# First stage of a one-core decoder trunk: filling products ahead of x, smaller first pieces, sums of squares behind the transposed x, low halves on GpSimd

## The chip, the core and the metric

The kernel runs on one core of a Trainium2 chip. TensorE (PE in the profile, its weight loads PEld), VectorE (DVE), ScalarE (ACT), GpSimd (POOL) and SyncE (SP) each work through a queue of their own in order and wait for one another by semaphores; 16 DMA engines move data. The metric is the device time of one execution in microseconds, as the median of several runs.

## The reference

The reference is a trunk of two residual layers on x of 256 tokens by 2048 features in float32, each followed by an MLP with a squared ReLU, and a norm at the end. Cut to what the change touches, the start of the first layer:

```python
D_MODEL = 2048; SEQ = 256; CONV_WIDTH = 31; EPS = 1e-6

def rms_norm(x, g):
    y = x * lax.rsqrt(jnp.mean(x * x, axis=-1, keepdims=True) + EPS)
    return y * g

def conv_module(h, w_in, b_in, dw, dw_b, ln_g, ln_b, w_out, b_out):
    u = h @ w_in + b_in                       # 2048 x 4096
    a, gate = jnp.split(u, 2, axis=-1)
    v = a * jax.nn.sigmoid(gate)
    v = depthwise causal convolution of v with dw, 31 taps, + dw_b
    v = jax.nn.silu(layer_norm(v, ln_g, ln_b))
    return v @ w_out + b_out

h = rms_norm(x, mix_norm[0])
x = x + conv_module(h, ...)
x = x + mlp(rms_norm(x, mlp_norm[0]), ...)    # then the state-space layer and its MLP
```

## The kernel before

**Precision by halves.** Products run in a one-pass float32 form that keeps fewer bits, so each operand is split: `hi` is the operand rounded to that form (an ACT copy, L117), `lo` is the operand minus `hi` (a subtraction, L119). A product is then three: hi by hi (L199), hi by the lo of the other side (L200), lo by hi (L201).

**Steps.** All weights are streamed as a list of steps, 1 MB each. `load` brings a step's chunk into one of three buffers `raw`; all chunks, and x, go through SP's queue in the order of the program (`fetch`, L91). `split` makes `hi` and `lo` of half a chunk; four buffers each for `hi` and `lo`, so splits run at most four halves ahead of the products, and a chunk can be asked for only when both halves of the chunk three before it have been split. The first two steps, halves 1 to 4 as counted in this text, are channel block 0 of `conv_w_in`, the next two, halves 5 to 8, are block 1. Each half feeds 24 products on TensorE (`mm_g`), so a block is 96. The set `pool_lo` says which steps have their `lo` made on GpSimd instead of VectorE: before the change, of `conv_in`, those from block 2 on.

**The first stage.** `setup` fetches x in four slices of 512 features, each followed by the half chunk of weights that multiplies it. TensorE transposes each slice (`to_features`, products `xt` at L242) with an identity matrix; ACT and VectorE scale it by the norm's gain `mix0` and split it into `hT` (L246, L247). The gain itself comes from a small transpose `mt` (L311) and a copy. The norm's factor per token is applied late: the sums of squares of x (`junk`, ACT at L259 and VectorE at L256) give `ssm`; GpSimd raises it to the power -1/2 (L274, `rstd`); two diagonal matrices `dg` and a product with ones (`bc`, L284) spread it over the partitions; and only the gate of block 0 (L434) uses it. In the same queue of GpSimd, behind that power, stand seven loads into one buffer `dwr`: biases and gains (L329) and the 31 convolution taps (L333). TensorE transposes them (`vt`, L335, and 16 small ones `dwt`, L341), and VectorE then starts the taps of block 0 (`cv`, L800), 30 steps per block.

**What sets the order.** The program is written once for all engines; a scheduler then sorts each engine's instructions by its own costs and by priorities (splits and gates are urgent), and inserts the waits. What an engine meets first in its queue is therefore not what stands first in the code, and any edit may move rows on all engines. `behind(ins)` tells the scheduler to place an instruction after another one.

Of the kernel before, what the change touches and what calls it, by code (L numbers as in the profile page):

```python
# [18 lines left out]
P = 128  # L19
# [17 lines left out]
class Trunk:  # L37
# [55 lines left out]
    def load(self, i, half=None):  # L93
        view, shape, _, _ = self.steps[i]
        for kind in self.before_load.pop(i, ()):
            self.table(*kind)
        if not half:
            self.raws[i] = self.w.tile(shape, F32, tag="raw", name="raw", bufs=3)
        raw = self.raws[i]
        nk = shape[1] // 2  # L100
        k = slice(0, shape[1]) if half is None else slice(half * nk, half * nk + nk)
        if len(shape) == 4:
            for j in range(shape[2]):
                self.fetch(raw[:, k, j, :], view[:, k, j, :])
        else:
            self.fetch(raw[:, k], view[:, k])
        self.loaded = i + 1

    def split(self, h, urgent=True):
# [5 lines left out]
        lo = self.w.tile([P, nk] + list(raw.shape[2:]), F32R, tag="lo", name="lo", bufs=4)  # L115
        with self.tc.high_priority(offset=URGENT if urgent else 0):
            self.nc.scalar.activation(hi, sl, AF.Copy)  # L117
            eng = self.nc.gpsimd if i in self.pool_lo else self.nc.vector
            ins = eng.tensor_tensor(out=lo, in0=sl, in1=hi.bitcast(F32), op=ALU.subtract)  # L119
            if i in self.pool_lo:  # L120
                self.pool_ins = ins
# [113 lines left out]
    def to_features(self, src, g, k0, n):  # L235

        nc = self.nc
        for k in range(k0, k0 + n, 2):
# [4 lines left out]
            for kk in range(2):  # L243
                gk = g[:, k + kk:k + kk + 1]
                h = self.hT(k + kk)
                nc.scalar.activation(h[:, 0, :], ps[:, kk, :], AF.Copy, scale=gk)  # L246
                nc.vector.scalar_tensor_tensor(out=h[:, 1, :], in0=ps[:, kk, :], scalar=gk,  # L247
                                               in1=h[:, 0, :].bitcast(F32), op0=ALU.mult, op1=ALU.subtract)
# [43 lines left out]
    def setup(self):  # L292
# [6 lines left out]
        for n in range(NS):  # L299
            s = slice(n * 512, (n + 1) * 512)  # L300
# [7 lines left out]
        nc.vector.memset(self.mhalf, -0.5)  # L308
        self.mix0 = const.tile([P, KB], F32, name="mix0")
# [5 lines left out]
        for n in range(NS):  # L315
            self.to_features(self.x, self.mix0, 4 * n, 4)
        for n in range(NS):
            self.sumsq(ssq, n, True)
# [80 lines left out]
    def conv_in(self):  # L399
# [5 lines left out]
        for c in range(KB):  # L405
            for kc in range(2):
# [9 lines left out]
                if c >= 2:  # L416
# [1095 lines left out]
```

## Time and profile before

| | |
|---|---|
| median of 3 runs | 2012.29 us (2011.23 to 2012.68) |
| the profiled execution: its time, its span | 2011.6 us, 2009.8 us |
| granted TensorE clock, mean | 0.996 |
| TensorE busy | 1977.3 us, 98% of the span |
| VectorE, ACT, GpSimd busy | 1399.2, 950.4, 280.6 us |
| DMA queue of SP | 384.85 MB, 60.9% of 16 engines over the span |
| first product of weights (L199) starts | 8.14 us |
| gate of block 0 (VectorE, L434) starts | 28.28 us |
| transposes of the taps (L341) start | 31.88 us |

The time of an execution is a little more than its span, which runs from the first to the last instruction. A row of the timeline gives start and length in us, engine, line, operation, the tile written and the tiles read, the shapes, the count, and in brackets the idle time of the engine ahead of it with what ended it. Groups give busy time and the mean of one in ns, then the idle time ahead. Matmul rows overlap in their length; the distance of their starts is what a product costs. Names are the program's: `xt` transposed x, `hT` its halves, `hi`, `lo`, `raw` as above, `dwr` the loaded constants, `acc` the accumulators.

### The profile page before, as it was taken

To read this page: it belongs to the slowest core of one execution; us is meant where nothing else is said; L and a number is where in the kernel's file an instruction comes from. 1 tells how busy PE (TensorE), PEld (TensorE's weight loads), DVE (VectorE), ACT (ScalarE), POOL (GpSimd) and SP (SyncE) were. 2 spreads that over 40 slices of the span, in tenths; PEclk is the share of its full clock that TensorE was granted. 3 is DMA by queue.
4 is the path that set the end of the run, shared out by engine and by line. 5 is a ranking of instruction groups with operands and counts; after the bars stand their busy time and mean duration, and the time that the engine had idled before them with its cause. 6 is when DMAs were issued, how large, how long until landed. Compare 5 with 4: busy or idle time off the path is not lost.

```text
span 2009.8 us, 28976 instructions
## 1 busy us (share of the span) xinstructions
PE 1977.3 (98%) x11640; PEld 1693.9 (84%) x11640; DVE 1399.2 (70%) x1905; ACT 950.4 (47%) x1172; POOL 280.6 (14%) x257
## 2 busy tenths in 40 slices
PE   8999999999999999999998999999999999999998
PEld 8999787888888888888886788888888888888887
DVE  7899899967776777776557747565556555565655
ACT  6444654444444544444443445554444444444444
POOL 3998301000000221222010000000000000000000
PEclk9999999999999999999999999999999999999999
DMA  8668458766866877877887865665656666575653
GB/s 233 190 173 217 141 199 262 229 228 191 262 189 188 220 235 245 263 249 241 321 287 269 285 210 184 194 181 186 199 187 191 188 189 195 184 223 185 198 189 126
DMA packets 317030, 428.49 MB, mean 213 GB/s; under 512 B 9761, under 2 KB 211553, under 8 KB 313537
## 3 DMA queue, kind: packets, MB, share of 16 engines
q1 hardware_dynamic: 301120, 384.85, 60.9%
q0 software_dynamic: 12352, 37.49, 6.2%
q10 hardware_dynamic: 3424, 4.30, 0.8%
q8 instruction: 91, 1.49, 0.3%
q14 instruction: 43, 0.35, 0.0%
HBM read 400.08 MB, written 34.91 MB: 216 GB/s over the span
## 4 chain that ended last, share of the span: by engine, by line
PE 92%; DVE 5%; DMA 1%; issue 1%; POOL 0%; ACT 0%; ACTq 0%; SPq 0%; POOLq 0%; DVEq 0%
PE acc L187 23%; PE acc L210 15%; PE acc L212 15%; PE acc L211 15%; PE acc L190 12%; PE acc L199 3%; PE acc L201 3%; PE acc L200 3%; DVE lo L119 1%; DVE S L791 1%; PE pk L472 1%; DMA raw<-in_conv_w_in_dram 1%; DVE ws L791 1%; PE kp L1084 0%; DMA raw<-in_mlp_w_up_dram 0%
## 5 line engine op out<-in xcount | busy, mean ns | idle before, releaser
L117 ACT ACTIVATE hi<-raw 128x1024 fp32r<-128x1024 f32 x672 | 711.8, 1060 | 968.0 <-PE acc L212 524.8
L119 DVE TENSOR_TENSOR lo<-raw,hi 128x1024 fp32r<-128x1024 f32 x612 | 747.6, 1223 | 522.2 <-ACT hi L117 513.2
L187 PE MATMUL acc<-hT,hi 128*128 128x512 f32 x2048 | 516.1, 394 | 3.0 <-DVE t L779 2.1
L187 PEld LDWEIGHTS acc<-hT,hi 128*128 128x128 f32 x2048 | 369.7, 189 | 72.2 <-DVE t L779 2.4
L210 PE MATMUL acc<-hi,rT 128*128 128x512 f32 x992 | 387.4, 391 | 0.0
L211 PE MATMUL acc<-lo,rT 128*128 128x512 f32 x992 | 386.3, 389 | 0.0
L212 PE MATMUL acc<-hi,rT 128*128 128x512 f32 x992 | 385.9, 389 | 0.0
L190 PEld LDWEIGHTS acc<-hT,lo 128*128 128x128 f32 x2048 | 279.5, 190 | 20.9 <-DVE lo L119 0.8
L190 PE MATMUL acc<-hT,lo 128*128 128x256 f32 x2048 | 286.1, 282 | 0.4 <-DVE lo L119 0.4
L210 PEld LDWEIGHTS acc<-hi,rT 128*128 128x128 f32 x992 | 186.2, 188 | 39.9 <-issue 1.8
L212 PEld LDWEIGHTS acc<-hi,rT 128*128 128x128 f32 x992 | 186.2, 188 | 39.1
L211 PEld LDWEIGHTS acc<-lo,rT 128*128 128x128 f32 x992 | 186.3, 188 | 37.8
L119 POOL TENSOR_TENSOR lo<-raw,hi 128x1024 fp32r<-128x1024 f32 x60 | 143.3, 2406 | 31.3 <-ACT hi L117 31.2
L199 PE MATMUL acc<-hT,hi 128*128 128x256 f32 x512 | 146.2, 286 | 1.1 <-ACT hi L117 1.0
L200 PE MATMUL acc<-hT,hi 128*128 128x256 f32 x512 | 145.7, 286 | 0.0
L201 PE MATMUL acc<-hT,lo 128*128 128x256 f32 x512 | 145.5, 286 | 0.0
L800 DVE SCALAR_TENSOR_TENSOR cv<-vT,dw,cv 128x256 f32<-128x256 f32 x348 | 141.2, 482 | 2.2 <-ACT cv L515 1.7
L791 DVE TENSOR_TENSOR x<-x,acc 128x1024 f32<-128x1024 f32 (+1 forms) x72 | 83.6, 1161 | 33.5 <-PE acc L212 22.8
L212 PE MATMUL acc<-hi,yT 128*128 128x512 f32 x256 | 101.7, 397 | 4.8 <-DVE yT L226 4.8
L210 PE MATMUL acc<-hi,yT 128*128 128x512 f32 x256 | 102.6, 401 | 1.3 <-ACT hi L117 1.3
L211 PE MATMUL acc<-lo,yT 128*128 128x512 f32 x256 | 101.2, 395 | 1.6 <-DVE lo L119 1.6
L199 PEld LDWEIGHTS acc<-hT,hi 128*128 128x128 f32 x512 | 98.9, 193 | 3.4 <-ACT hi L117 1.7
(274 smaller groups left out, 1732.7 us busy)
## 6 DMA issues: line engine op xcount, KB each, us to landing
raw<-in_mlp_w_up_dram SPq DMA_DIRECT2D x128, 1024.0 KB, 5.8
raw<-in_mlp_w_down_dram SPq DMA_DIRECT2D x128, 1024.0 KB, 5.2
raw<-in_ssm_w_glu_dram SPq DMA_DIRECT2D x32, 1024.0 KB, 5.5
raw<-in_conv_w_in_dram SPq DMA_DIRECT2D x60, 512.0 KB, 5.6
raw<-in_conv_w_out_dram SPq DMA_DIRECT2D x16, 1024.0 KB, 5.2
Vd<-bv POOLq DMA_DIRECT2D x16, 512.0 KB, 4.9
Md<-Kd POOLq DMA_DIRECT2D x32, 256.0 KB, 7.9
Wt<-Wd SPq DMA_DIRECT2D x8, 1024.0 KB, 8.6
```

The source lines that it names most:

```text
L117: self.nc.scalar.activation(hi, sl, AF.Copy)
L119: ins = eng.tensor_tensor(out=lo, in0=sl, in1=hi.bitcast(F32), op=ALU.subtract)
L187: mm(accs[m], lhsT=hi[:, kk, cs[m]], rhs=xT(k0 + kk), start=first and kk == 0, stop=False)
L190: mm(accs[m][:, 0:T], lhsT=lo[:, kk, cs[m]], rhs=xT(k0 + kk)[:, 0, :], start=False, stop=last and kk == 3)
L199: mm(accs[m], lhsT=hi[:, kk, c], rhs=x[:, 0, :], start=first and kk == 0, stop=False)
L200: mm(accs[m], lhsT=hi[:, kk, c], rhs=x[:, 1, :], start=False, stop=False)
L201: mm(accs[m], lhsT=lo[:, kk, c], rhs=x[:, 0, :], start=False, stop=last and kk == 3)
L210: mm(acc[:, b, :], lhsT=ak[:, 0, t], rhs=hi[:, kk, :], start=first and kk == 0, stop=False)
L211: mm(acc[:, b, :], lhsT=ak[:, 0, t], rhs=lo[:, kk, :], start=False, stop=False)
L212: self.mm_last = mm(acc[:, b, :], lhsT=ak[:, 1, t], rhs=hi[:, kk, :], start=False, stop=last and kk == 1)
L791: self.nc.vector.tensor_tensor(out=out, in0=a, in1=b, op=op)
L800: return self.nc.vector.scalar_tensor_tensor(out=out, in0=a, scalar=s, in1=b, op0=op0, op1=op1)
```

## The change

It has five parts. (1) Eight products of ones with ones, of 128 columns, are put ahead of the first transposes; their result is not used. (2) The first slice of x and its half chunk of weights come in two pieces each, and the first half is split in two pieces. (3) The sums of squares are placed behind the last instructions of the last slice's `hT`, on ACT and VectorE. (4) `pool_lo` takes in all steps of `conv_in` but the first: halves 3 to 8 have their `lo` on GpSimd. (5) `to_features` returns its last two instructions, for part 3.

```diff
-    def load(self, i, half=None):
+    def load(self, i, half=None, part=None):
...
-        if not half:
+        if not (half or part):
             self.raws[i] = self.w.tile(shape, F32, tag="raw", name="raw", bufs=3)
...
+        if part is not None:
+            k = slice(part * nk // 2, (part + 1) * nk // 2)
...
+        n = nk // 2 if h == 0 else nk
         with self.tc.high_priority(offset=URGENT if urgent else 0):
-            self.nc.scalar.activation(hi, sl, AF.Copy)
             eng = self.nc.gpsimd if i in self.pool_lo else self.nc.vector
-            ins = eng.tensor_tensor(out=lo, in0=sl, in1=hi.bitcast(F32), op=ALU.subtract)
+            for k in (slice(k, k + n) for k in range(0, nk, n)):
+                self.nc.scalar.activation(hi[:, k], sl[:, k], AF.Copy)
+                ins = eng.tensor_tensor(out=lo[:, k], in0=sl[:, k], in1=hi[:, k].bitcast(F32), op=ALU.subtract)
...
         for n in range(NS):
+            if n == 0:
+                for p in range(2):
+                    s = slice(p * 256, (p + 1) * 256)
+                    self.fetch(self.x[:, :, s], xv[:, :, s])
+                    self.load(0, 0, p)
+                continue
             s = slice(n * 512, (n + 1) * 512)
...
+        warm = self.acc2("warm")[:, 0, 0:P]
+        for _ in range(8):
+            nc.tensor.matmul(warm, lhsT=self.ones, rhs=self.ones, start=True, stop=True)
...
         for n in range(NS):
-            self.to_features(self.x, self.mix0, 4 * n, 4)
-        for n in range(NS):
-            self.sumsq(ssq, n, True)
+            ins = self.to_features(self.x, self.mix0, 4 * n, 4)
+        with self.behind(ins[0]), self.behind(ins[1]):
+            for n in range(NS):
+                self.sumsq(ssq, n, True)
...
-                if c >= 2:
+                if c or kc:
                     self.pool_lo.add(len(self.steps))
```

What the scheduler made of it, at three places. GpSimd's queue from the identity matrix on (`ssm` is the mean of squares, `dwr` the loaded constants), before:

```order
masks.py:199 AFFINE_SELECT ident<-ident 128x128
L274 TENSOR_TENSOR rstd<-ssm,mhalf 128x2
L329 DMA dwr<-in_conv_b_in_dram 32x128
L329 DMA dwr<-in_conv_dw_b_dram 16x128
L333 DMA dwr<-in_conv_dw_dram 31x2048
L119 TENSOR_TENSOR lo<-raw,hi 128x1024 x12
```

and with the change:

```order
masks.py:199 AFFINE_SELECT ident<-ident 128x128
L123 TENSOR_TENSOR lo<-raw,hi 128x1024 x4
L279 TENSOR_TENSOR rstd<-ssm,mhalf 128x2
L344 DMA dwr<-in_conv_b_in_dram 32x128
L344 DMA dwr<-in_conv_dw_b_dram 16x128
L348 DMA dwr<-in_conv_dw_dram 31x2048
L123 TENSOR_TENSOR lo<-raw,hi 128x1024 x13
```

Four low halves, 3 to 6, now stand ahead of the power and the loads (rows of the loads in between, and of memsets, are left out); the next two, 7 and 8, stand behind them.

TensorE's queue where the constants are transposed, behind products of the second block, before:

```order
L201 MATMUL acc<-hT,lo 128x256
L335 MATMUL vt<-ident,dwr 128x112
L199 MATMUL acc<-hT,hi 128x256
L200 MATMUL acc<-hT,hi 128x256
L341 MATMUL dwt<-ident,dwr 128x31 x16
```

and with the change:

```order
L204 MATMUL acc<-hT,hi 128x256
L289 MATMUL bc<-dg,ones 128x256
L350 MATMUL vt<-ident,dwr 128x112
L356 MATMUL dwt<-ident,dwr 128x31 x16
L203 MATMUL acc<-hT,hi 128x256
```

`vt` stood behind 144 products and `dwt` behind 149; both now stand behind 146, with `bc`, which stood behind 81, right ahead of them.

ACT's queue around the sums of squares (`junk`) and the diagonal `dg`, before:

```order
L259 ACTIVATE junk,ssq<-x 128x512
L246 ACTIVATE hT<-xt,mix_104 128x256
L117 ACTIVATE hi<-raw 128x1024
L246 ACTIVATE hT<-xt,mix_104 128x256 x4
L117 ACTIVATE hi<-raw 128x1024 x2
L282 ACTIVATE dg<-ident,rstd 128x128
```

and with the change:

```order
L250 ACTIVATE hT<-xt,mix_116 128x256 x4
L264 ACTIVATE junk,ssq<-x 128x512
L122 ACTIVATE hi<-raw 128x1024 x2
L264 ACTIVATE junk,ssq<-x 128x512 x3
L122 ACTIVATE hi<-raw 128x1024 x3
L287 ACTIVATE dg<-ident,rstd 128x128
```

The four sums of squares, one per slice of x before, now come after the last `hT`, three of them behind the high halves 5 and 6, and `dg` comes behind the high halves 7 to 9.

More of the change, by code (lines that the diff above doesn't have):

```diff
@@ L245, in to_features @@
                 h = self.hT(k + kk)
-                nc.scalar.activation(h[:, 0, :], ps[:, kk, :], AF.Copy, scale=gk)
-                nc.vector.scalar_tensor_tensor(out=h[:, 1, :], in0=ps[:, kk, :], scalar=gk,
-                                               in1=h[:, 0, :].bitcast(F32), op0=ALU.mult, op1=ALU.subtract)
+                hi = nc.scalar.activation(h[:, 0, :], ps[:, kk, :], AF.Copy, scale=gk)
+                lo = nc.vector.scalar_tensor_tensor(out=h[:, 1, :], in0=ps[:, kk, :], scalar=gk,
+                                                    in1=h[:, 0, :].bitcast(F32), op0=ALU.mult, op1=ALU.subtract)
+        return hi, lo
     def sumsq(self, ssq, n, both=False):
```

## The prediction

> **What bounds the kernel now.** I read the page first, then TensorE's waits, then the first 40 us by stage and by engine.
>
> ```profile
> PE 1977.3 (98%) x11640; PEld 1693.9 (84%) x11640; DVE 1399.2 (70%) x1905; ACT 950.4 (47%) x1172; POOL 280.6 (14%) x257
> PE 92%; DVE 5%; DMA 1%; issue 1%; POOL 0%; ACT 0%; ACTq 0%; SPq 0%; POOLq 0%; DVEq 0%
> ```
>
> TensorE is busy for 98% of the span and carries 92% of the chain that ended last. So only what TensorE loses counts, and a microsecond it loses early is not made up later. The change is in the start; some windows of the first 40 us (columns: length, busy time and count of PE, PEld, DVE, ACT, POOL, then clock, DMA share, GB/s):
>
> ```profile
> 5.00:10.00 5.00, 3.83 (x16) 3.43 (x17) 3.15 (x8) 3.76 (x9) 0.00 (x0) 1.00 1.06 332
> 20.00:30.00 10.00, 10.00 (x83) 9.94 (x82) 7.16 (x11) 5.43 (x8) 4.41 (x12) 1.00 1.15 258
> 30.00:40.00 10.00, 10.00 (x91) 9.83 (x90) 5.43 (x13) 8.20 (x21) 4.74 (x2) 1.00 0.99 257
> ```
>
> TensorE is full in the later two, and the DMA engines in all three (a share of about 1). What can be won is before 13.4 us:
>
> ```profile
> 8.14 0.58 PE L199 MATMUL acc<-hT,hi 128*128 128x256 f32 x1 [1.04 <-ACT hi L117]
> 8.74 1.91 PE L242 MATMUL xt<-ident,x 128*128 128x128 f32 x8
> 12.79 0.41 PE L200 MATMUL acc<-hT,hi 128*128 128x256 f32 x1
> 13.01 0.41 PE L201 MATMUL acc<-hT,lo 128*128 128x256 f32 x1
> 13.43 0.28 PE L200 MATMUL acc<-hT,hi 128*128 128x256 f32 x1
> 13.55 0.28 PE L201 MATMUL acc<-hT,lo 128*128 128x256 f32 x1
> ```
>
> Products start 0.22 us apart until 13 us and 0.12 us apart from 13.43 on: TensorE starts at half speed. The stretch from 8.74 to 13.43, 4.7 us, would take half of that at full speed. With the wait of 1.04 us before the first product, the front of the program holds at most 2.35 + 1.04 = 3.4 us.
>
> **The change, part by part.** *Filling products and smaller first pieces.* They aim at those 3.4 us. The filling runs on TensorE from about 1.2 us, when it has nothing else: no cost but a delay of the small transpose for `mix0`, which stands behind it, and of the copy that ACT's first `hT` needs. The smaller pieces put three more issues on SP's queue, each as long as this one, with the time from issue to landing of the first chunks below it:
>
> ```profile
> 0.74 0.44 SPq L91 DMA_DIRECT2D x<-in_x_dram  x1
> raw<-in_conv_w_in_dram SPq DMA_DIRECT2D x8, 256.0 KB, 6.8
> ```
>
> Three times about 0.5 us of issuing lie beside 6.8 us in which earlier bytes are still on their way, so later chunks land as before; without that cover it would be 1.5 us. Bounds for the front alone: nothing, or 3.4 us won. I take neither, because of the next part.
>
> *Low halves on GpSimd.* The chunks of the first two channel blocks, halves 3 to 8 in order, had their low halves on VectorE and now have them on GpSimd:
>
> ```profile
> L119 DVE TENSOR_TENSOR lo<-raw,hi x8: 1217/1225/1227, 8.1 to 28.9; 128x1024 fp32r<-128x1024 f32 x8
> 30.86 4.74 POOL L119 TENSOR_TENSOR lo<-raw,hi 128x1024 fp32r<-128x1024 f32 x2 [6.45 <-ACT hi L117]
> 13.37 1.06 ACT L117 ACTIVATE hi<-raw 128x1024 fp32r<-128x1024 f32 x1 [0.41 <-DMA raw<-in_conv_w_in_dram]
> 16.58 1.06 ACT L117 ACTIVATE hi<-raw 128x1024 fp32r<-128x1024 f32 x1 [0.46 <-DMA raw<-in_conv_w_in_dram]
> 20.20 2.01 ACT L117 ACTIVATE hi<-raw 128x1024 fp32r<-128x1024 f32 x2 [1.10 <-DMA raw<-in_conv_w_in_dram]
> ```
>
> One costs 1.23 us on VectorE and 2.37 us on GpSimd. Each can start only when ACT has the high half, and ACT waits for the weights to land (at 13.4, 16.6 and, for halves 5 and 6, 20.2 us). The bytes ahead of them are the same after the change and the DMA engines are full, so these landings stay. GpSimd then ends half 3 at 13.37 + 1.06 + 2.37 = 16.8, half 4 at 16.58 + 1.06 + 2.37 = 20.0, and halves 5 and 6 at 20.20 + 1.06 + 4.74 = 26.0 us. TensorE needs 24 products of 0.12 us = 2.9 us per half, so after 26.0 it is through half 6, 144 products, at about 28.9; in the profile it is there at 31.08, where the row of `vt` below starts, with the broadcast `bc` (0.4 us) already done. That is a lead of 1.8 us, however much more the front won, since half 6 sets it.
>
> *What is queued behind them on GpSimd.* The power that makes `rstd`, and behind it the seven loads of the constant vectors and convolution taps (`dwr`), now stand after these four low halves:
>
> ```profile
> 19.46 0.71 POOL L274 TENSOR_TENSOR rstd<-ssm,mhalf 128x2 f32<-128x2 f32 x1 [18.14 <-DVE ssm L272]
> 20.11 0.73 POOL L329 DMA_DIRECT2D dwr<-in_conv_b_in_dram  x1
> 23.23 0.53 POOL L333 DMA_DIRECT2D dwr<-in_conv_dw_dram  x1
> 31.08 0.26 PE L335 MATMUL vt<-ident,dwr 112*128 112x112 f32 x1
> 31.88 1.18 PE L341 MATMUL dwt<-ident,dwr 31*128 31x31 f32 x16
> 32.98 0.38 PE L201 MATMUL acc<-hT,lo 128*128 128x256 f32 x1
> ```
>
> The power started at 19.46, the last load was issued 3.77 us after that. Now the power starts at 26.0 us, 6.5 us later. The sums of squares, now behind the last transposed x, are no reason for more:
>
> ```profile
> L259 ACT ACTIVATE junk<-x 128x512 f32<-128x512 f32 x4 | 2.5, 630 | 2.6 <-DMA x<-in_x_dram 2.6
> L259 ACT ACTIVATION_READ_ACCUMULATOR junk<-x 128x1 f32 x4 | 0.8, 196 | 0.0
> ```
>
> ACT's last three come after the two high halves of 20.20, at 22.2 + 3 x 0.83 = 24.7 us, and two short VectorE steps follow. The last load is then issued at 26.0 + 3.77 = 29.8 us. TensorE's transposes of these loads (`vt`, `dwt`) stand after 146 products, where they stood after 144 and 149; TensorE reaches them at 28.9 + 0.2 + 0.4 (for `bc`, now right ahead of them) = 29.5 us and must wait, with every product queued behind. (`bc` could come later, since ACT's `dg` now stands behind the high half 9; that costs nothing of its own as long as the loads, behind `bc`, are later still.)
>
> *How long the loads take to land.* Issue to landing on GpSimd's queue, as a median or as min/median/max:
>
> ```profile
> dwr<-in_conv_dw_dram POOLq DMA_DIRECT2D x1, 248.0 KB, 7.4
> DMA to landing us min/median/max: 5.8/6.3/7.4
> DMA to landing us min/median/max: 3.3/4.0/5.0
> Kd<-zero POOLq DMA_DIRECT2D x4, 224.0 KB, 3.2
> ```
>
> The second row is all seven `dwr` loads, the third the four loads of `bo`, 256 KB each, at 101 to 123 us. The 7.4 us were taken with the DMA engines full; after the change the sixth chunk of weights can be asked for only when half 6 has been split at 26.0, and the seventh only after half 8, so about one chunk of 1 MB is in flight beside the loads. That is nearest to `bo`; since seven loads stand one behind the other I take its longest, 5.0, and keep 3.2 and 7.4 as bounds. The taps land at 29.8 + 5.0 = 34.8 us. `vt` and the 16 small transposes took 0.1 + 1.1 us: done at 36.0. Three products fewer are behind TensorE by then (3 x 0.12 = 0.36), so 36.4 against 32.98: **3.4 us lost**; by the bounds 1.6 to 5.8.
>
> *The clock after the wait.* TensorE would stand idle from 29.5 to 34.8, 5.3 us. Two waits of the profile show what follows:
>
> ```profile
> 308.52 0.50 PE L211 MATMUL acc<-lo,sT 128*128 128x512 f32 x1 [2.23 <-DVE lo L119]
> 308.85 0.39 PE L212 MATMUL acc<-hi,sT 128*128 128x512 f32 x1
> 309.08 0.40 PE L210 MATMUL acc<-hi,sT 128*128 128x512 f32 x1
> 1087.72 0.79 PE L212 MATMUL acc<-hi,yT 128*128 128x512 f32 x1 [4.83 <-DVE yT L226]
> 1088.31 0.63 PE L210 MATMUL acc<-hi,yT 128*128 128x512 f32 x1
> 1092.11 0.39 PE L210 MATMUL acc<-hi,yT 128*128 128x512 f32 x1
> ```
>
> After 2.23 us of idle time products are 0.23 us apart as before; after 4.83 us nine of them take the 3.8 us from 1088.31 to 1092.11, 0.42 each, which lost 9 x 0.2 = **1.8 us**. I take 1.8; it is nothing if the wait stays near 2 us. The Trainium skill ("TensorE: Matmul & The Clock Gate", Part 1) says that a window of about 3.4 us without work halves the clock and a busy one of that length restores it; these two waits agree, and by the rule the loss would be the same 1.7 us.
>
> *The rest.* VectorE gets 6 x 1.23 us back, in windows where it was not full (7.2 of 10 us, 5.4 of 10 us) and where nothing of TensorE's waited for it: worth nothing. Later in the program a few rows change places; the largest waits of TensorE there are these, and I leave them as they are, with 1.5 us either way in the range:
>
> ```profile
> PE acc L211 <- DVE lo L119: 3.9, 2, 2.2
> PE acc L187 <- DVE t L779: 2.1, 1, 2.1
> ```
>
> *Sum.* 3.4 + 1.8 = 5.2 us slower. The profiled execution took 2011.6 us (span 2009.8), so 2016.8; it lies 0.7 us under the median of the three runs, 2012.3, which makes **2017.5 us**. A change under 0.2%, 4.0 us, is what a measurement of this kernel cannot tell from none.
>
> **The rivals.**
>
> *The loads land soon.* At 3.2 us the taps are there at 33.0, the loss is 1.6 us, and with an idle time of 3.5 us the clock may hold: 2013.9, no measurable change. For it: one small group of transfers on this queue did land in 3.2 us. Against it: those are copies of zeros at a time of little traffic, and the same seven loads took 5.8 us or more. The Trainium skill ("DMA: Bandwidth & Descriptors", Anatomy of one DMA) gives 2.0 us plus the bytes at 436 GB/s for this path, by my estimate 2.6 us for 248 KB and a loss of 1.0 us; no load in this profile was that quick.
>
> *The lead is kept (the other side).* If the constants are there when TensorE reaches them, it keeps the lead of 1.8 us: 2010.5. It decides from a landing at 29.5, and gain and loss are equal where the taps land at 31.4 us, 1.6 us after their issue as I have it. So GpSimd would have to be done with half 6 some 2 us or more earlier than 26.0, which the landing at 20.2 and 2.37 us a piece do not allow. Even with nothing in the way, 3.4 us is below what can be told.
>
> *A second wait.* The column sums for the layer norm stand earlier in TensorE's order: the second from the start after 496 products instead of 526, 30 x 0.12 = 3.6 us. The last tap they wait for is VectorE's, and this is how far it was ahead:
>
> ```profile
> 75.11 0.48 DVE L800 SCALAR_TENSOR_TENSOR vT<-vT,dw,cv 128x256 f32<-128x256 f32 x1
> 79.13 0.62 PE L527 MATMUL stat<-vT,ones 128*32 128x256 f32 x2
> ```
>
> 3.5 us: about used up by the move. Should VectorE, which starts its taps behind the same `dwt`, come 3 us later than in the profile, 3 us more are lost: 2020.5. Against it: VectorE's order moved too, with the last tap of the first block after 46 instead of 55 of its steps.
>
> **How the numbers follow.** The stall with a fallen clock 0.64, the quick landing 0.19, the lead kept 0.06, the second wait 0.09, something else 0.02. The first reaches from 4.2 (landing in 4.0 us) to 7.8 us (in 7.4 us with 2.0 for the clock), or 2020.1; a tenth of it falls under 4.0. The range takes in the quick landing and most of the second wait, and leaves out the lead: 2012.0 to 2020.5. Faster by over 0.2%: 0.04, which is what exceeds my bound on the front. Within 0.2%: 0.19 + 0.05 + 0.07 = 0.31. Slower: 0.65.
>
> **What would show it.** Right, if in the new profile GpSimd's fourth low half ends at about 26 us, the power follows at once, TensorE has a wait of some 5 us for a `dwr` load ahead of `vt` or `dwt`, and the products behind it are 0.21 us apart for some 3.5 us. The front is right if products begin near 7 us and the halves 3 to 6 are waited for on GpSimd. I am wrong if the power starts well before 26 us, if the taps land within 3.5 us of their issue, if the clock holds through the wait, or if TensorE later has waits that the profile of before does not have.

## The result, and the profile after

The changed kernel took 2020.4 us (median of 5 executions, 2019.51 to 2025.75) against 2012.29 us: slower, by a factor of 1.0047 (95% interval 1.0033 to 1.0061). The forecast was 2017.5 us. The direction was right, and so was the kind of the loss: a wait of TensorE for the late loads, and a fallen clock behind it. Its size was not: the step that puts the power at 26.0 us failed, as worked out further down. The loss is about half as large again as forecast where a second wait stays away, and more where it comes.

The profiled execution is the longest of the five, 2025.75 us with a span of 2024.0. The busy time by engine on its page:

```profile
PE 1985.2 (98%) x11656; PEld 1700.3 (84%) x11656; DVE 1405.5 (69%) x1900; ACT 950.8 (47%) x1173; POOL 295.8 (15%) x263
```

These hardly differ from before: a page's shares cannot show 14 us in 2024. I therefore use a lag below: the start of a TensorE instruction minus the start of the same instruction in the kernel before, both from the span's start. The lag of a single row also holds any move of that row in the order. In this execution it is 1.0 us at 30 us of the time before, 9.3 us at 40, still 9.4 at 100, 14.6 at 112 and 14.3 at the end. So there are two losses, 8.3 us at 30 to 40 us and 5 us at 106 to 112, and nothing in between is made up.

The first loss, in the timeline of GpSimd, VectorE and TensorE. Low halves 5 and 6, the power and the issue of the last load on GpSimd; two of VectorE's squares; and TensorE from the broadcast on:

```profile
23.66 5.61 POOL L123 TENSOR_TENSOR lo<-raw,hi 128x1024 fp32r<-128x1024 f32 x2 [0.64 <-PE acc L205]
30.37 0.71 POOL L279 TENSOR_TENSOR rstd<-ssm,mhalf 128x2 f32<-128x2 f32 x1 [1.10 <-DVE ssm L277]
34.14 0.53 POOL L348 DMA_DIRECT2D dwr<-in_conv_dw_dram  x1
...
24.22 2.79 DVE L261 SCALAR_TENSOR_TENSOR junk<-x 128x512 f32<-128x512 f32 x1
26.94 2.88 DVE L261 SCALAR_TENSOR_TENSOR junk<-x 128x512 f32<-128x512 f32 x1
...
32.37 0.60 PE L289 MATMUL bc<-dg,ones 128*128 128x256 f32 x2
37.27 0.42 PE L350 MATMUL vt<-ident,dwr 112*128 112x112 f32 x1 [4.30 <-DMA dwr<-in_mlp_norm_dram]
37.63 1.90 PE L356 MATMUL dwt<-ident,dwr 31*128 31x31 f32 x16
39.46 0.58 PE L203 MATMUL acc<-hT,hi 128*128 128x256 f32 x1
39.84 0.41 PE L204 MATMUL acc<-hT,hi 128*128 128x256 f32 x1
44.96 0.37 PE L204 MATMUL acc<-hT,hi 128*128 128x256 f32 x1
45.16 0.28 PE L205 MATMUL acc<-hT,lo 128*128 128x256 f32 x1
```

This is the chain that the prediction describes: low halves, then the power, then the loads, then TensorE waiting at `vt`, then products 0.21 us apart until 45 us (25 of them from 39.84 to 44.96). The broadcast `bc` starts at 32.37 with no idle time of TensorE ahead of it, so neither the low halves nor the power hold TensorE there; only the load behind it does. Two things in the chain were not foreseen: half 6 ends at 29.27 instead of 26.0, and the power waits another 1.10 us for the mean of squares, since two of VectorE's squares took 2.79 and 2.88 us where one of the four took 0.68.

The second loss, by the waits of TensorE and the timeline of VectorE and GpSimd:

```profile
PE stat L542 <- DVE vT L572: 3.8, 1, 3.8
...
112.56 7.88 DVE L572 TENSOR_TENSOR vT<-vT,shift 128x1024 f32<-128x1024 f32 x1
...
112.31 2.41 POOL L403 TENSOR_TENSOR x<-x,bo 128x1024 f32<-128x1024 f32 x1
114.67 4.69 POOL L123 TENSOR_TENSOR lo<-raw,hi 128x1024 fp32r<-128x1024 f32 x2
119.31 0.56 POOL L401 DMA_DIRECT2D bo<-in_conv_b_out_dram  x1
```

The centre subtraction of the layer norm took 7.88 us; the same one took 1.67 us before. It ends at 120.44, 1.08 us after GpSimd's three operations, which end at 119.36.

### The profile page after: what moved, and what is told of

It is laid out like the page before. It is cut to its first block, busy times and chain, and to the rows that moved or that the text cites. A ratio compares the mean times of both kernels' runs of the same rounds, so it can differ in the third digit from the quotient of the medians.

```text
span 2024.0 us, 29016 instructions
## 1 busy us (share of the span) xinstructions
PE 1985.2 (98%) x11656; PEld 1700.3 (84%) x11656; DVE 1405.5 (69%) x1900; ACT 950.8 (47%) x1173; POOL 295.8 (15%) x263
## 4 chain that ended last, share of the span: by engine, by line
PE 91%; DVE 6%; issue 1%; DMA 1%; SPq 0%; POOL 0%; ACT 0%; ACTq 0%; POOLq 0%; DVEq 0%
PE acc L191 23%; PE acc L214 15%; PE acc L216 15%; PE acc L215 15%; PE acc L194 12%; PE acc L203 3%; PE acc L205 3%; PE acc L204 3%; DVE lo L123 1%; DVE S L806 1%; PE pk L487 1%; DVE ws L806 1%; PE kp L1099 0%; DMA raw<-in_mlp_w_up_dram 0%; DMA raw<-in_conv_w_in_dram 0%
## 5 line engine op out<-in xcount | busy, mean ns | idle before, releaser
L122 ACT ACTIVATE hi<-raw 128x1024 fp32r<-128x1024 f32 (+1 forms) x673 | 711.8, 1059 | 964.3 <-PE acc L216 526.9
L123 DVE TENSOR_TENSOR lo<-raw,hi 128x1024 fp32r<-128x1024 f32 (+1 forms) x607 | 740.2, 1221 | 523.4 <-ACT hi L122 522.2
L123 POOL TENSOR_TENSOR lo<-raw,hi 128x1024 fp32r<-128x1024 f32 x66 | 158.4, 2411 | 47.0 <-ACT hi L122 46.3
```

Of the source, the lines that this page charges most:

```text
L122: self.nc.scalar.activation(hi[:, k], sl[:, k], AF.Copy)
L123: ins = eng.tensor_tensor(out=lo[:, k], in0=sl[:, k], in1=hi[:, k].bitcast(F32), op=ALU.subtract)
```

## The experiments

**The changed kernel again.**

> The changed kernel once more. Two losses stand in its first profile: 8.3 us at 30 to 38 us (the wait for the constant vectors, the cold clock behind it) and 5.0 us at 107 to 122 us (a wait for a centre subtraction of 7.88 us on VectorE, which took 1.67 us before). Theory A, the first loss belongs to the change and the second to that one execution: the new profile has the wait for the vectors of 4 to 5 us again, no centre subtraction above 3 us, and a span of about 2018.5 us. Theory B, both belong to the change: the subtraction takes over 6 us again, and the span is 2022 us or more.

Measured: 2026.07 us (2019.66 to 2029.23, six executions), 1.0069 [1.0057, 1.0081].

```profile
PE vt L350 <- DMA dwr<-in_mlp_norm_dram: 4.5, 1, 4.5
...
111.18 10.76 DVE L572 TENSOR_TENSOR vT<-vT,shift 128x1024 f32<-128x1024 f32 x1
...
110.92 2.41 POOL L403 TENSOR_TENSOR x<-x,bo 128x1024 f32<-128x1024 f32 x1
113.27 4.70 POOL L123 TENSOR_TENSOR lo<-raw,hi 128x1024 fp32r<-128x1024 f32 x2
117.91 0.56 POOL L401 DMA_DIRECT2D bo<-in_conv_b_out_dram  x1
118.49 2.35 POOL L403 TENSOR_TENSOR x<-x,bo 128x1024 f32<-128x1024 f32 x1
```

Theory B holds: the first loss is there again (a wait of 4.5 us for the loads, lag 7.9 us at 40 us), and of the second 7.8 us stay (lag 16.6 at 108 us, 15.8 from 140 us to the end), against 5.0 in the first profile. This time the subtraction ended at 121.94, 1.10 us after the fourth operation on GpSimd, 120.84 (the DMA issue between them is not counted). Both belong to the change; the second varies between executions. Of its eleven times, five lie between 2019.5 and 2020.7 and six between 2023.8 and 2029.2.

**Filling and pieces alone; then one part back at a time.** Three kernels. The first has the low halves back on VectorE and the sums of squares where they were, so that only the filling and the pieces are left; the second has only the low halves back, the third only the sums. The edit for the low halves comes first, then the one for the sums:

```diff
-                if c or kc:
+                if c >= 2:
...
-            ins = self.to_features(self.x, self.mix0, 4 * n, 4)
-        with self.behind(ins[0]), self.behind(ins[1]):
-            for n in range(NS):
-                self.sumsq(ssq, n, True)
+            self.to_features(self.x, self.mix0, 4 * n, 4)
+        for n in range(NS):
+            self.sumsq(ssq, n, True)
```

> Only the filling products and the smaller pieces: low halves of the second to fourth step back on VectorE, sums of squares where they were before. Theory A (the loss is the late load of the constants, and that comes from the two other parts): no wait for a load behind 158 products; products begin near 9 us as in the changed kernel, 1 to 2 us later than before, of which the later pace of the halves hides a part: 2011.5 to 2014. Rival (the front wins, and the other parts eat the gain): products begin earlier than in the changed kernel, 2009 to 2010.5. Rival (the front itself loses what the changed kernel loses): 2016 or more.

> The changed kernel with the low halves of halves 3 to 8 back on VectorE; the sums of squares stay behind the transposed x. One low half, that of half 9, now stands ahead of the power on GpSimd, and TensorE meets the broadcast behind 190 products, the vectors behind 192. My prediction's step (low halves on GpSimd are what makes the loads late) in its plain form: nothing of the loss is left, 2011 to 2013. Theory A (the loads are late whenever the power is late, whoever makes it so): half 9 is split at about 31 us, the power comes at about 33, the last vectors land at about 41, TensorE reaches them at about 37 to 38: a wait of 3 to 4 us and a cold clock, 2016 to 2019. Theory C (GpSimd's low halves slow VectorE, and that is the loss): 2011 to 2013, with no square of VectorE above 1 us.

> The changed kernel with the sums of squares where they were; halves 3 to 8 keep their low halves on GpSimd. One low half stands ahead of the power, and TensorE meets the vectors and taps behind 76 products already. Theory A: power at about 17 us, the last load issued at about 21, landed at 27 to 28 with the DMA engines full; TensorE gets there at about 21: a wait of 5 to 7 us, then a cold clock; half 6 would have been ready at 26, so 4 to 7 us are lost against before, 2016 to 2019.5. Theory D (the two parts are only bad together, each alone is harmless): 2011 to 2013.5.

Measured, with the lag at some times of the kernel before:

| kernel | median us | ratio [95%] | lag at 30 | 40 | 100 | 140 | 356 | 400 | end |
|---|---|---|---|---|---|---|---|---|---|
| change, first profile | 2020.4 | 1.0047 [1.0033, 1.0061] | 1.0 | 9.3 | 9.4 | 14.3 | 14.0 | 14.2 | 14.3 |
| filling and pieces | 2020.28 | 1.0041 [1.0029, 1.0053] | 0.6 | 0.6 | 0.0 | 1.1 | 0.0 | 7.6 | 7.0 |
| low halves back | 2021.75 | 1.0050 [1.0038, 1.0062] | -0.4 | 3.8 | 3.7 | 4.8 | 9.9 | 10.2 | 9.8 |
| sums back | 2024.12 | 1.0061 [1.0048, 1.0074] | 8.6 | 7.2 | 7.7 | 6.9 | 9.9 | 9.0 | 13.0 |

No part undone brings the time back. In the first, the front loses nothing worth naming, as the prediction has it, and yet 7.6 us go at 356 to 400 us, where no part of the change is; no theory had that. In the second, the loads are late without any of halves 3 to 8 on GpSimd: half 9, which was on GpSimd all along, now stands ahead of the power. In the third the power is early, but the scheduler has moved `vt` up to 76 products. The rows are the power on GpSimd and TensorE's wait, for low halves back and then for sums back:

```profile
32.90 0.71 POOL L279 TENSOR_TENSOR rstd<-ssm,mhalf 128x2 f32<-128x2 f32 x1
PE vt L350 <- DMA dwr<-in_mlp_norm_dram: 1.8, 1, 1.8
...
19.55 0.71 POOL L279 TENSOR_TENSOR rstd<-ssm,mhalf 128x2 f32<-128x2 f32 x1
PE vt L349 <- DMA dwr<-in_mlp_norm_dram: 4.1, 1, 4.1
```

Theory A is right in kind in both: TensorE waits for the loads whichever part makes them late, or meets them early. Its sizes are not right: the waits are 1.8 and 4.1 us, where it had 3 to 4 and 5 to 7, and both times lie above its ranges. A part of those times is lost later: with the low halves back the lag goes from 4.8 us at 140 us to 10.7 at 280, with one wait of 2.9 us for VectorE among it; with the sums back it goes from 6.9 at 140 us to 13.0 at the end. These later losses were not traced to a cause, so neither end time is the price of a part. Low halves on GpSimd are one way to late loads, not the only one. Theories C and D fall. In these three profiles the centre subtraction took 2.17, 1.62 and 1.50 us; which part of the change brings it together with GpSimd's addition is not shown.

**Why filling and pieces alone lose 7 us.** In VectorE's order, laid beside that of the kernel before, about 150 rows at 350 us and later stand elsewhere. With one filling product fewer that part of the order is the old one again:

```diff
-        for _ in range(8):
+        for _ in range(7):
```

> Filling products and smaller pieces alone, as in the run with those two parts, but with seven filling products instead of eight: the scheduler's order on VectorE from 350 us on is then that of the kernel before, where with eight it differed by some 150 rows. Theory A (that run's loss of 7 us lies in VectorE's order at 380 to 400 us, not in the front): 2010.5 to 2013. Rival B (the front costs 6 to 8 us by itself, through late landings or ACT): 2017 to 2021, the same as with eight.

Measured: 2012.45 us, 1.0003 [0.9994, 1.0013]. The lag is about 1.0 us from 30 to 140 us and 0.1 at 400. TensorE's waits for the MLP's accumulators, and the busy times from 370 to 400 us (length, busy time and count of PE, PEld, DVE, ACT, POOL, clock, DMA share, GB/s), with eight fillings and then with seven:

```profile
PE acc L191 <- DVE t L793: 7.8, 4, 3.5
370.00:400.00 30.00, 25.29 (x137) 21.83 (x136) 30.00 (x41) 12.37 (x15) 2.53 (x3) 0.94 0.73 224
```

```profile
PE acc L191 <- DVE t L793: 3.0, 2, 2.1
370.00:400.00 30.00, 29.16 (x167) 25.46 (x166) 30.00 (x41) 15.53 (x19) 2.08 (x2) 1.00 0.88 267
```

VectorE is full in both, 30.00 of 30 us. What differs is the order of its work. The operation `t` that frees TensorE's accumulator starts at 367.7, 380.3 and 395.3 us with eight fillings, with 10, 9 and 10 operations on the next layer's tables (L805) ahead of each; with seven it starts at 365.3, 375.4 and 389.1, with 9, 4 and 9. Theory A holds: one product on an idle TensorE at 1 us decides over 7 us at 390, through the scheduler's order. The changed kernel as a whole happens not to have this loss (lag 14.0 at 356, 14.2 at 400).

**Six fillings alone.** The kernel before with six of them:

```diff
+        warm = self.acc2("warm")[:, 0, 0:P]
+        for _ in range(6):
+            nc.tensor.matmul(warm, lhsT=self.ones, rhs=self.ones, start=True, stop=True)
```

> The kernel before with six filling products and nothing else; all engines keep their order but for one place. Theory A (the landing of half 6 sets the pace of the first 30 us): the products may start at full speed, but the lag is within 0.5 us of nothing at 30 us; 2011 to 2012.5. Rival (the half-speed stretch of 8.7 to 13.4 us is really lost time): 1.5 to 2.3 us are won and stay won: 2009.5 to 2010.5.

Measured: 2011.61 us, 0.9999 [0.9990, 1.0009]. TensorE's products lead by 0.93 us until 14.0 us; from 20 to 140 us they are 0.13 to 0.15 us behind. Time and lag are as theory A has them, its reason is not: the lead is lost to a wait for VectorE's `hT`, and no wait for a half of the weights follows. With seven fillings and smaller pieces, too, the lead of 0.5 to 1.3 us ends at a wait for VectorE's `hT`. The two waits, of this run and then of that one:

```profile
14.09 0.63 PE L246 MATMUL xt<-ident,x 128*128 128x128 f32 x4 [0.63 <-DVE hT L251]
20.85 0.39 PE L204 MATMUL acc<-hT,hi 128*128 128x256 f32 x1 [0.94 <-DVE hT L251]
```

Behind these, no wait of TensorE up to the end of half 6 is above 0.15 us in either run.

**The table of ACT's functions.** The change moved ACT's first operation behind the first weights, and its table load with it. Here a small copy of a constant comes first:

```diff
         nc.vector.memset(self.mhalf, -0.5)
+        nc.scalar.activation(self.small.tile([P, NB], F32, tag="tl", name="tl", bufs=1), self.mhalf, AF.Copy)
```

> The changed kernel with one more small ACT copy of a constant at the start, which waits for no load, so that the table of ACT's functions is fetched then; all other orders are those of the changed kernel. Theory A (the table load was held up by the first weights and cost the front 1.2 us, but the front is not what decides): the first high half at about 5.7 us instead of 6.9, the first product at about 7.7 instead of 8.95; the lag against before falls by about 1.2 us at 9 to 25 us and is the same 8 to 9 us at 40 us; 2019 to 2021, or up to 2026 where the centre subtraction is held. Rival (the front carries through): the lag is lower by 1.2 us to the end.

Measured: executions of 2018.17, 2018.31, 2026.52 and 2028.34 us, 1.0064 [1.0039, 1.0089]. Table load and first product, of the changed kernel and then of this one:

```profile
5.60 1.28 ACT L122 ACT_TABLE_LOAD   x1 [5.60 <-DMA raw<-in_conv_w_in_dram]
8.95 0.58 PE L203 MATMUL acc<-hT,hi 128*128 128x256 f32 x1 [1.85 <-ACT hT L250]
```

```profile
1.23 1.28 ACT L320 ACT_TABLE_LOAD   x1 [1.23 <-PEq L1517]
7.41 0.39 PE L203 MATMUL acc<-hT,hi 128*128 128x256 f32 x1 [0.18 <-ACT hT L250]
```

The first product is 1.5 us earlier, and the lag at 40 us is 7.9 us, as in the repeated run of the change. That is as theory A has it, but it is little evidence: two profiles of the changed kernel itself differ by 1.4 us there (9.3 and 7.9), and the executions of 2018.17 and 2018.31 lie 1.2 to 2.5 us below the five of the changed kernel between 2019.5 and 2020.7. So the rival, that the 1.2 us carry through, is not excluded. In this profile the centre subtraction was not held:

```profile
111.15 1.22 DVE L573 TENSOR_TENSOR vT<-vT,shift 128x1024 f32<-128x1024 f32 x1
111.16 3.47 POOL L404 TENSOR_TENSOR x<-x,bo 128x1024 f32<-128x1024 f32 x1 [0.30 <-DMA bo<-in_conv_b_out_dram]
```

GpSimd's addition waited 0.30 us for its load; VectorE came 0.01 us ahead of it, kept its 1.22 us, and the addition took 3.47 instead of 2.4. That so small a lead decides over the second loss is not shown: in a section of the second program below VectorE also stood 0.01 us ahead, and was held for 5.75 us.

**The loads by another way.** Three kernels. First through SyncE's queue; then at the head of GpSimd's queue; then the same with whole first pieces.

```diff
-            with self.behind(self.pow_ins):
-                nc.gpsimd.dma_start(out=rows[r:r + n, :], in_=ap.rearrange("(k p) -> k p", p=P))
+            self.fetch(rows[r:r + n, :], ap.rearrange("(k p) -> k p", p=P))
```

```diff
-            with self.behind(self.pow_ins):
-                nc.gpsimd.dma_start(out=rows[r:r + n, :], in_=ap.rearrange("(k p) -> k p", p=P))
+            nc.gpsimd.dma_start(out=rows[r:r + n, :], in_=ap.rearrange("(k p) -> k p", p=P))
```

(the load of the taps alike in each)

> The changed kernel with the seven loads of constants and taps put into SyncE's queue behind the first four half chunks of weights, instead of GpSimd's behind the power. Broadcast, vectors and taps stand behind 146 products as in the changed kernel. The price of the late loads alone. Theory A (the loads are what TensorE waits for): no wait for a load at 33 us, no cold products behind it, lag against the kernel before at 40 us 1.5 to 4.5 us instead of 8 to 9 (seven more issues of 0.5 us ahead of the third chunk are the upper part); the end 2013 to 2016, and more only by the centre subtraction. Theory B (the power itself, or GpSimd's low halves, hold TensorE as long): lag at 40 us still 7 us or more, 2019 or more.

> The changed kernel with the seven loads of constants and taps at the head of GpSimd's queue, ahead of its low halves, instead of behind the power; low halves and sums of squares as in the changed kernel. Broadcast, vectors and taps now stand behind 130 products. VectorE's order at 350 us and later is that of the run with eight fillings and smaller pieces (the same 154 rows differ). Theory A (the late loads are the first loss, VectorE's order in the later stage is a loss of its own): no wait for a load; TensorE reaches the broadcast at about 30.4 us and waits 1 to 2 us for the power; lag against the kernel before at 40 us 2 to 4 us instead of 8 to 9; then 6 to 8 us more at 370 to 400 us; the end 2019 to 2022. Theory B (the low halves and the power hold TensorE anyway): lag at 40 us 7 us or more. Theory E (VectorE's order in the later stage does not matter, the run with eight fillings lost its 7 us by something else): nothing is lost at 370 to 400 us, the end 2013 to 2016.

> The same with x and the first weights fetched and split in whole pieces as before; broadcast, vectors and taps stand behind 143 products, and VectorE's order at 350 us and later is that of the kernel before. Theory A: TensorE reaches the broadcast at about the time the power is through, nothing is waited for above 1 us, lag at 40 us 0 to 2.5 us, nothing at 370 to 400 us; 2011.5 to 2014.5, with up to 8 us more where a centre subtraction is held behind GpSimd. Theory B: 2019 or more. So low halves on GpSimd and sums behind the transposed x cost next to nothing once the loads do not stand behind them.

| kernel | median us | ratio [95%] | lag at 20 | 30 | 40 | 100 | 356 | 400 | end |
|---|---|---|---|---|---|---|---|---|---|
| on SyncE's queue | 2025.72 | 1.0071 [1.0056, 1.0086] | 0.9 | 13.7 | 14.1 | 13.5 | 13.7 | 13.9 | 13.8 |
| head of GpSimd's queue | 2024.65 | 1.0065 [1.0050, 1.0080] | 6.3 | 8.8 | 7.5 | 7.5 | 5.8 | 13.6 | 13.2 |
| the same, whole pieces | 2016.15 | 1.0027 [1.0016, 1.0039] | 5.7 | 5.0 | 5.4 | 4.8 | 4.5 | 4.7 | 4.1 |

The first meets theory B's sign (a lag of 14.1 us at 40 us), but neither theory has its cause: the loads are no longer waited for, but the weights queued behind them are. TensorE's wait:

```profile
PE acc L203 <- ACT hi L122: 9.4, 1, 9.4
```

In the trace's DMA events of this kernel, the load of the taps was issued on SyncE's queue at 17.35 us and landed at 30.68, after 13.3 us, and the next half chunks of weights landed 14 and 16 us after their issue. The Trainium skill ("DMA: Bandwidth & Descriptors", Why a DMA increments its semaphore by 16 and not by 1) says that a transfer from this queue uses as many engines as divide its outer dimension, up to 16; 31 rows would then go through one engine. The trace agrees: the 31 packets of 8 KB that make up this load ran one after another from 18.72 to 30.16 us, and of the 1024 packets of the half chunk behind it 960 had started by 22.0 us, the last 64, one sixteenth, only from 30.17 on.

The other two paid in the front, 6 us at 20 us, since the loads now go ahead of x and the first weights; later TensorE waits another 4.8 and 2.4 us for a high half. But from 20 to 40 us, with the low halves of 3 to 6 on GpSimd and the power as late as in the change (31.05 in the last), they lose 1.2 us and nothing (5.7 to 5.4), where the changed kernel loses 7.8 (1.5 to 9.3) and its repetition 7.5. A window of the changed kernel; the broadcast with the loads at the head of the queue; then the power, the broadcast and the same window with whole pieces as well:

```profile
30.00:40.00 10.00, 5.70 (x43) 5.06 (x42) 2.86 (x8) 3.88 (x5) 9.63 (x15) 0.75 0.51 139
...
36.41 0.60 PE L289 MATMUL bc<-dg,ones 128*128 128x256 f32 x2
...
31.05 0.73 POOL L279 TENSOR_TENSOR rstd<-ssm,mhalf 128x2 f32<-128x2 f32 x1 [1.11 <-DVE ssm L277]
35.94 0.60 PE L289 MATMUL bc<-dg,ones 128*128 128x256 f32 x2
30.00:40.00 10.00, 10.00 (x89) 9.67 (x89) 5.62 (x10) 6.26 (x10) 8.96 (x5) 1.00 0.59 162
```

In the window of 30 to 40 us the changed kernel's TensorE is busy for 5.7 us at a clock of 0.75; with the loads at the head and whole pieces it is 10.0 us at 1.00. So early loads are not waited for, and the clock stays up. But these two runs do not test theory B. TensorE is late by then and reaches the broadcast at 36.41 and 35.94 us, 3.5 to 4 us later than in the changed kernel, when the power is long through. The first of them, with a lag of 7.5 us at 40 us, even meets theory B's sign, and both miss theory A's times and lags. What speaks against theory B is the changed kernel itself: its broadcast starts at 32.37 with no idle time ahead, and the 4.30 us come behind it, for a load. By my estimate from its rows, without that wait it would have been through `dwt` at 32.97 + 1.2 = 34.2 us, with a lag of 1.5 us instead of 9.3. So the late loads are the first loss. The second kernel also has the order of VectorE with 154 rows moved, and lost 7.8 us at 356 to 400 us, as theory A said and theory E denied.

**VectorE and GpSimd beside one another.** Two programs of their own, with no computation of the reference (they copy x to the output).

> A program of its own, which leaves the whole computation out (it copies x to the output) and measures VectorE and GpSimd beside one another. Each section starts both engines together: GpSimd with a row of subtractions of 128x1024, all operands in SBUF (2.4 us each), VectorE with one short operation that reads PSUM and then the one in question. The lock theory (an operation of VectorE with two operands in SBUF waits until a running operation of GpSimd has ended, and GpSimd's next one waits for it): the subtraction of 128x1024, 1.22 us alone, ends about 1.1 us behind the end of one of GpSimd's, so it takes 2 to 3 us beside one, and 5 us or more where GpSimd's follow without a gap and it misses its turn; an operation with one operand in PSUM keeps its time. The sharing theory (both are slowed evenly while they overlap): VectorE's takes 1.5 to 2.5 us and GpSimd's 3 to 4 us, with no tie to the end of GpSimd's. The rival from the traces' other side (what holds VectorE is a semaphore or its own queue): all sections show 1.22 us.

Rows of VectorE and GpSimd: two subtractions with both operands in SBUF alone; one subtraction of GpSimd and one of VectorE together; four operations with one operand in PSUM beside four of GpSimd; a copy from SBUF to SBUF beside them; two subtractions beside GpSimd memsets:

```profile
6.59 2.48 DVE L63 TENSOR_TENSOR vo<-va,vb 128x1024 f32<-128x1024 f32 x2
...
18.13 2.34 POOL L75 TENSOR_TENSOR go<-ga,gb 128x1024 f32<-128x1024 f32 x1
18.76 2.79 DVE L63 TENSOR_TENSOR vo<-va,vb 128x1024 f32<-128x1024 f32 x1
...
45.74 2.85 DVE L66 SCALAR_TENSOR_TENSOR vo<-va,ps 128x512 f32<-128x512 f32 x4
67.35 2.26 DVE L72 COPY vo<-va 128x1024 f32<-128x1024 f32 x1
77.79 2.48 DVE L63 TENSOR_TENSOR vo<-va,vb 128x1024 f32<-128x1024 f32 x2
```

The lock theory holds: 18.76 + 2.79 = 21.55 is 1.08 us after GpSimd's end at 18.13 + 2.34 = 20.47. An operand in PSUM keeps the time (four in 2.85 us, 0.69 each), and a memset of GpSimd holds nobody. Not expected: a plain copy in SBUF, 0.69 us alone, took 2.26. The Trainium skill ("SBUF — State Buffer", Who interferes with whom) states this rule, an exclusive lock that is held for a whole instruction, for operations of VectorE with two SBUF inputs and for copies that use both of its ports; every row here agrees. But in all these sections VectorE came in after one operation of GpSimd, never after three or four.

> A program of its own again (the computation left out, x copied to the output), now with the very shapes of the held centre subtraction: GpSimd adds a broadcast row to x (128x2x512), then two subtractions, a DMA issue, and the addition again, or the same with plain subtractions; VectorE's centre subtraction (128x4x256 in place, a broadcast row) or a plain one comes 0 to 0.7 us behind the start of the first. Theory F (GpSimd's addition with the broadcast row is what lets VectorE miss its turn): beside it the centre subtraction takes 5 us or more in at least some sections and ends 1.1 us behind GpSimd's DMA issue or behind the whole row; beside plain subtractions it takes at most 3.6 us. Theory G (the form of VectorE's operation decides): it is the centre form that waits 5 us beside either row, and the plain form never. Theory H (neither: what was queued or in flight in the whole kernel decides): no section shows more than 3.6 us, and the reason stays open.

VectorE and GpSimd, in three sections: a DMA issue, the addition of a broadcast row, then subtractions; the same without the DMA issue; the DMA issue, then plain subtractions:

```profile
31.15 5.75 DVE L87 TENSOR_TENSOR vt<-vt,sh 128x1024 f32<-128x1024 f32 x1
31.16 2.35 POOL L90 TENSOR_TENSOR xg<-xg,b 128x1024 f32<-128x1024 f32 x1
33.46 5.63 POOL L97 TENSOR_TENSOR go<-ga,gb 128x1024 f32<-128x1024 f32 x2
...
141.64 3.30 DVE L87 TENSOR_TENSOR vt<-vt,sh 128x1024 f32<-128x1024 f32 x1
80.28 3.64 DVE L87 TENSOR_TENSOR vt<-vt,sh 128x1024 f32<-128x1024 f32 x1
```

Theory F in part: where the addition follows a DMA issue, as in the kernel, VectorE misses its first turn and takes 5.4 to 6.0 us, in all seven sections in which it came once the DMA issue had begun, with the centre form and with the plain one. It then comes in after the second operation, not after the whole row as the theory had it; and without the DMA issue, or with a plain subtraction first, it misses none (3.2 to 3.6 us). Theory G falls, and so does theory H, which had no section above 3.6 us. Why VectorE came in only after three and four operations in the two profiles of the whole kernel stays open.

## Why the prediction was right and wrong

- *What bounds the kernel*: right. TensorE never regained what it lost; the lag stands at 9.3 to 9.4 us from 40 to 100 us.
- *Filling and smaller pieces are worth nothing*: right in the sum (1.0003 and 0.9999), but not for the reason given, that half 6 sets the lead. In the two runs of this part alone the lead was lost before, to waits for VectorE's `hT` at 14.09 and 20.85 us. Products also did not begin near 7 us but at 8.95, because the table load of ACT came to wait for the weights.
- *Half 6 is split at 26.0 us and the power follows at once*: this is the step that failed. The power started at 30.37 us, 4.37 us late. Of these, 3.27 are half 6, which ended at 29.27, and 1.10 a wait for the sums of squares.
- *These landings stay* (the part of it that put half 6 too early): by the trace's DMA events half 3's weights landed at 14.84 us instead of 13.28, half 4's at 18.03 instead of 16.50, the third chunk, halves 5 and 6, at 21.61 instead of 20.09. That is as much as the prediction gives for the three extra issues "without that cover"; with seven fillings and the pieces alone the third chunk was 1.1 us late (21.18), so most of it belongs to the pieces. Besides, ACT came to the high half of 3 at 17.13 us, where I had 13.37, so GpSimd was done with half 4 at 23.01 instead of 20.0, and low halves 5 and 6 took 5.61 us, not 4.74. ACT's high halves 3, then 5 and 6, and GpSimd's low halves 3 and 4:

```profile
17.13 1.05 ACT L122 ACTIVATE hi<-raw 128x1024 fp32r<-128x1024 f32 x1
22.53 2.00 ACT L122 ACTIVATE hi<-raw 128x1024 fp32r<-128x1024 f32 x2
...
18.26 4.75 POOL L123 TENSOR_TENSOR lo<-raw,hi 128x1024 fp32r<-128x1024 f32 x2 [16.94 <-ACT hi L122]
```

- *The sums of squares are no reason for more*: this part of the step failed too. I took VectorE's squares at their time alone. Beside GpSimd's low halves three of four took 1.11, 2.79 and 2.88 us instead of 0.68, so the power waited 1.10 us after half 6. The two parts of the change are in each other's way through the port that VectorE and GpSimd share, a rule of the Trainium skill ("SBUF — State Buffer", Who interferes with whom) that speaks against this change and that I did not weigh.
- *The loads land 5.0 us after the last issue*: mis-sized the other way; the taps landed at 37.50 us, 3.35 after their issue at 34.14 (the trace's DMA events; the page's groups say 3.4), near the lower bound of 3.2. It gave back 1.65 of the 4.37 us.
- *Stall and clock*: the mechanism is right, the size is not. TensorE waited 4.30 us, forecast 5.3; but it arrived at 32.97 instead of 29.5. The products behind `dwt` began at 39.46, forecast 36.0. The small transposes ran slowly too, 1.90 us instead of 1.1, and 25 products were slow where I counted nine: 25 x 0.09 = 2.3 us against 1.8. TensorE was slow from 37.27 to 45.16 us, 7.9 us, where I had some 3.5.
- *The sum*: half 6 3.27, the sums of squares 1.10, the landing -1.65, the small transposes 0.8 and the slow products 0.5 make 4.0 us more than the forecast 5.2. That is 9.2, against a lag of 9.3 in this profile; the lag was 7.9 in the repeated run and in the run with the early table load.
- *The rivals*: the loads landed about as soon as the first rival has it, but a late issue made up for it. The lead was not kept; when TensorE stood at `vt`, the last load had not been issued. *A second wait* came true at the column sums of the layer norm, though at a later one (it ends at 120.5 us), and not by its mechanism: not VectorE's taps were late, its subtraction was held by GpSimd. It was worth 5.0 and 7.8 us, not 3, and by the times it came in about half of the executions; 0.09 was too little.
- *What would show it*: of the signs for being right, the wait ahead of `vt` and the products 0.21 us apart came, half 6 at 26 us and the power at once did not. Of the signs for being wrong two came: the taps landed within 3.5 us of their issue, and a later wait, 3.8 us at `stat`, is new. The sign for the front did not come either: TensorE waited once for one of the low halves on GpSimd, 0.23 us at 20.71.
- *Later rows are left as they are, 1.5 us either way*: right for this change from 140 us on, and by luck. Four of its relatives lost 6 to 8 us later on: two in which about 150 rows of VectorE's order stand elsewhere, and the two with one part put back, where the reason was not traced.

## What to carry to other kernels

Where a scheduler sets the order, an experiment that undoes one part of an edit is a new program: compare its order on each engine, and its lag curve, before its time is put down to that part. When work moves to GpSimd, list what VectorE runs beside it with two operands in SBUF, and what stands behind it in GpSimd's own queue; here both ended at the same power. A load that is needed soon should not wait behind computed work on its queue, nor go ahead of the first weights, nor on the queue of the weights itself, where its 31 rows went one by one: each way cost about 4 us or more.

## What the runs showed of the hardware

- The port: an operation of VectorE with two SBUF operands ends 1.08 to 1.10 us (for 128x1024) after the end of a GpSimd operation, and can miss turns; one of 1.22 us took 7.88 and 10.76.
- A wait of 4.3 us on TensorE was followed by 1.9 us of slow transposes and 5.1 us of products at half speed; the granted clock was 0.75 from 30 to 40 us and 0.74 from 40 to 50.
- A table load of ACT takes over the wait of the operation behind it: 1.28 us that were free at 1.23 us were on the path at 5.60.
- The same load of 248 KB in 31 rows took 13.3 us on SyncE's queue, its packets one after another, and 3.2 to 8.0 us on GpSimd's.
